# Gated delta rule beside two dense projections: the recurrence of eight heads as two staggered chains of four

## The chip, the cores and the metric

The kernel runs on one core of one Trainium2 chip. Its metric is the device time of one execution in microseconds, as the median of three runs. A core has TensorE (PE, with its weight loads shown apart as PEld), VectorE (DVE), ScalarE (ACT), GpSimd (POOL) and SyncE (SP, which here only issues DMAs). Each engine works through its own instructions in a fixed order.

## The reference, cut to what matters

One decoder layer: RMSNorm, one wide input projection, three mixers beside each other (gated DeltaNet, stick-breaking attention, memory attention), each projected to 1024 channels, gated and summed, then an output projection, residual and RMSNorm. The part in question is the recurrence of the DeltaNet mixer and what it feeds:

```
def step(s, xs):                      # 8 heads, dk = dv = 128
    q_n, w_n, u_n, k_n, a_n, last_n = xs
    v_new = u_n - einsum('bhcd,bhde->bhce', w_n, s)
    o = einsum('bhcd,bhde->bhce', q_n, s) + einsum('bhcs,bhse->bhce', a_n, v_new)
    s = s * exp(last_n) + einsum('bhcd,bhce->bhde', k_n, v_new)
    return s, o
...
o_dn = merge_heads(rmsnorm(o_dn, dn_norm_g)) * silu(dn_z)
merged = g_dn * (o_dn @ w_br_dn) + g_sb * (o_sb @ w_br_sb) + g_m * (o_m @ w_br_mem)
```

The state `s` of a head at chunk n needs chunk n-1 of the same head, and nothing of the other heads.

## The kernel before, in words

All data are 32 bit. The big projections are done as three products each of a high and a low part (`mm3`, and the three matmuls of `branch`), over tiles of 128 by 512. Up to about 1220 us of the execution the kernel does the input projection, the triangular solves, memory attention and stick-breaking attention. Then comes the stage in question. It has two things to do at once:

- **The dense branches** (`branch`, L1125 and on). For each of 8 blocks of 128 output channels and both halves of the 1024 tokens: first the memory branch (`y_ym`, contraction over 2 tiles), then the stick-breaking branch (`y_ysb`, over 8 tiles), at last the delta branch (`y_ydn`, over 8 tiles, one for each head of the recurrence). The sums gather in `mer`. Each result takes one of four PSUM banks of the tag `y` until DVE has multiplied it with its gate `gt` (L1143, or L1145 and L1146).
- **The recurrence** (`recurrence`), over 8 chunks n of 128 tokens and, within a chunk, two groups g of four heads. One chunk of one group is a chain: `kS` (L775, keys times state), `vb` (L777, DVE), `Tr` (L783, the solved triangle times `vb`), `vn` (L785, ACT), then `o` (L790 and L791, the output) and `dS` (L795, the change of state), `S` (L798, DVE), and a last part that norms `o` (ACT L808, POOL L809 to L811, DVE L812), transposes it (`oT`, L815), multiplies it with the gate `zt` (L816) and splits it into `odnh` and `odnl` (L143, L144), which `y_ydn` reads. `kS`, `Tr`, `o` and `dS` go to three PSUM banks of the tag `wk`. Each of their 128 by 128 matmuls is in plain 32 bit and shows as two matmuls in the trace.

What orders the two against each other: `recurrence` is a generator that yields between the parts of a chain, and `branch` calls `beside3` after every second contraction tile (40 calls in the memory and stick-breaking branches), which advances the generator to a share `RP` = 1.05 of its 65 steps, some 1.7 steps for each call. What is left after the last call is drained before the delta branch. The program so recorded is then ordered once more, when it is built, by a scheduler with its own timing model: each engine's instructions get a fixed order, and may stand elsewhere than in the program. Loads are issued by SP, in order too. A load into a buffer that is still read waits on SP for its release, and all later loads wait behind it.

The loads of a chunk (`loads`) are `kt`, `vb`, `tt` (three pieces), `kd`, `qd`, `at` and `zt`. `kd`, `qd` and `zt` have one buffer for both groups, `kt`, `vb` and `at` have two.

At the start of the stage the last tiles of stick-breaking attention (`av`, `aTp`, `aTl`) still run. The memory branch's input is `om` times `zm` (L1119, in `raw_m`), split into `oh_m` and `ol_m`, its weights are split into `w_wbm`, and the attention's outputs are loaded into `raw_sb` and split into `oh_sb` and `ol_sb`, through four `raw` buffers.

Of the kernel before, what the change touches and what calls it, by code (L numbers as in the profile page):

```python
# [11 lines left out]
F32 = mybir.dt.float32  # L12
F32R = mybir.dt.float32r
AF = mybir.ActivationFunctionType
ALU = mybir.AluOpType
# [4 lines left out]
P = 128  # L20
T = 1024
NT = 8
KC = 8
H = 8
# [13 lines left out]
def hybrid_block(ctx, tc, x, mem, norm_g, mem_norm_g, wq, wv0, wba, convw, a_log, dt_bias,  # L38
                 dn_g, wmk, wmv, wbd, wbs, wbm, wout, final_g, out):
    nc = tc.nc  # L40
    ve, sc, gp, pe, sy = nc.vector, nc.scalar, nc.gpsimd, nc.tensor, nc.sync
# [14 lines left out]
    cst = pool("cst", 1)  # L56
# [16 lines left out]
    def psum(tag, name):  # L73
        if tag == "X" and "X" not in banks["tags"]:
            tag = "z"
        if tag in MM:
            return mmp.tile([P, 512], F32, tag=tag, bufs=MM[tag], name=name)
        return banks["pool"].tile([P, 512], F32, tag=tag, bufs=banks["tags"][tag], name=name)
# [3 lines left out]

    ident = cst.tile([P, P], F32, name="ident")
    make_identity(nc, ident)
    tri = cst.tile([P, P], F32, name="tri")
    gp.memset(tri, 1.0)
    gp.affine_select(out=tri, in_=tri, compare_op=ALU.is_ge, fill=0.0, base=0,
                     pattern=[[1, P]], channel_multiplier=-1)
    ones = cst.tile([P, P], F32, name="ones")
    gp.memset(ones, 1.0)  # L90
    mhalf = cst.tile([P, 8], F32, name="mhalf")
    gp.memset(mhalf, -0.5)
    cw = cst.tile([P, 24, 4], F32, name="cw")
# [3 lines left out]
    def tab(n):  # L97
        if n not in tabs:
            tabs[n] = cst.tile([P, H, NT], F32, name="tab_" + n)
        return tabs[n]  # L100
# [163 lines left out]
    bat = cst.tile([P, NT, 16], F32, name="bat")  # L264
# [131 lines left out]
    v_st.close()  # L396


    beta, G, nG, eG, elast, dec = (tab(n) for n in ("beta", "G", "nG", "eG", "elast", "dec"))
    nr2, r1, r3, eq = tab("nr2"), tab("r1"), tab("r3"), tab("eq")  # L400
    SS = dict(c=None)

# [336 lines left out]
    def recurrence(ep, odn):  # L739
# [10 lines left out]
        def loads(n, g):  # L750
            kt = ld(kt_d, n, g, "kt") if n else None
            vb = ld(vb_d, n, g, "vb")
            tt, hs = tts[g], slice(g * 4, g * 4 + 4)
            for b in range(2):
                q = slice(b * 64, b * 64 + 64)
                sy.dma_start(out=tt[q, :, q], in_=td_d[b, hs, n].rearrange("h j i -> j h i"))
            sy.dma_start(out=tt[0:64, :, 64:P], in_=xx_d[n, :, hs, :])
            kd = ld(kd_d, n, g, "kd", 1) if n < NT - 1 else None
            qd = ld(qd_d, n, g, "qd", 1) if n else None
            at = ld(at_d, n, g, "at")  # L760
            zt = ep.tile([P, 4, P], F32, tag="zt", bufs=1, name=f"zt_{n}_{g}")
            sy.dma_start(out=zt, in_=zf_d[g * 4:g * 4 + 4, :, n * P:n * P + P].rearrange("h d t -> d h t"))
            return kt, vb, tt, kd, qd, at, zt

        ahead = loads(0, 0)
        yield
        for n in range(NT):
            for g in range(2):
                hs = range(4)
                kt, vb, tt, kd, qd, at, zt = ahead or loads(n, g)  # L770
                ahead = None
                if n:
                    o = psum("wk", f"kS_{n}_{g}")
                    for h in hs:
                        pe.matmul(o[:, h * P:h * P + P], kt[:, h, :], S[:, g * 4 + h, :], start=True, stop=True)  # L775
                    for h in hs:
                        ve.scalar_tensor_tensor(out=vb[:, h, :], in0=o[:, h * P:h * P + P],  # L777
                                                scalar=r3[:, g * 4 + h, n:n + 1], in1=vb[:, h, :],
                                                op0=ALU.mult, op1=ALU.add)
                    yield  # L780
                o = psum("wk", f"Tr_{n}_{g}")
                for h in hs:
                    pe.matmul(o[:, h * P:h * P + P], tt[:, h, :], vb[:, h, :], start=True, stop=True)  # L783
                vn = ep.tile([P, 4, P], F32, tag="vn", bufs=1, name=f"vn_{n}_{g}")
                sc.activation(vn, o.rearrange("p (h c) -> p h c", h=4), AF.Copy)  # L785
                yield
                oo = psum("wk", f"o_{n}_{g}")
                for h in hs:
                    if n:
                        pe.matmul(oo[:, h * P:h * P + P], qd[:, h, :], S[:, g * 4 + h, :], start=True, stop=False)  # L790
                    pe.matmul(oo[:, h * P:h * P + P], at[:, h, :], vn[:, h, :], start=(n == 0), stop=True)  # L791
                if n < NT - 1:
                    o = psum("wk", f"dS_{n}_{g}")
                    for h in hs:
                        pe.matmul(o[:, h * P:h * P + P], kd[:, h, :], vn[:, h, :], start=True, stop=True)  # L795
                    for h in hs:
                        if n:
                            ve.scalar_tensor_tensor(out=S[:, g * 4 + h, :], in0=S[:, g * 4 + h, :],  # L798
                                                    scalar=elast[:, g * 4 + h, n:n + 1],
                                                    in1=o[:, h * P:h * P + P], op0=ALU.mult, op1=ALU.add)  # L800
                        else:
                            ve.tensor_copy(S[:, g * 4 + h, :], o[:, h * P:h * P + P])
# [10 lines left out]
                o = psum("tr", f"oT_{n}_{g}")  # L813
# [2 lines left out]
                ve.tensor_tensor(out=zt, in0=o.rearrange("p (h c) -> p h c", h=4), in1=zt, op=ALU.mult)  # L816
                split([t[:, g * 4:g * 4 + 4, n * P:n * P + P] for t in odn], zt)
                yield

    SOLVE, MEM, COMB, RECUR = 1 + 1 + 62 + 8, 4 * 6, 16, 1 + 16 * 4  # L820

# [62 lines left out]

    b_st = sub()
    bp = pool("B", 1, stack=b_st, side="right")
    def hn(t):
        return t.rearrange("p h n -> p n h")

# [405 lines left out]
```

## Time and profile before

| | |
|---|---|
| median of 3 runs | 1628.51 us (1625.81 to 1630.97) |
| the profiled execution | 1621.97 us, its span from first to last instruction 1620.3 us |
| PE busy | 1549.0 us, 96% of the span |
| weight loads | 1299.1 us, 80% |
| DVE, ACT, POOL busy | 1180.3 us (73%), 819.6 us (51%), 312.5 us (19%) |
| granted TensorE clock, mean | 0.986 of full speed |
| moved by DMA | 223.32 MB, mean 138 GB/s |

PE is busy nearly throughout, so the few places in which it stands still are what can be taken away. A share of busy time over the whole span hides them; the rows below look at the stage from 1235 to 1442 us alone.

### The profile page before, as it was taken

Reading aid. Unit: us, or ns where it says so; the run is one execution under the profiler, and the core shown is the slowest. Engines: PE = TensorE matmul, PEld = TensorE weight load, DVE = VectorE, ACT = ScalarE, POOL = GpSimd, SP = SyncE. Lnnn points to the kernel's source line nnn. Section 1 sums busy time; section 2 is a strip of 40 time slices with the busy share of each in tenths; the row PEclk is TensorE's granted clock in tenths of the full one; section 3 lists DMA queues with packets and bytes.
Section 4 is the critical chain, followed back from the end, with each engine's and each line's share of the span. In section 5 each row is a group of like instructions: output and inputs, shape, how many; then the busy total and the mean of one; then the engine's idle time right before and its main releaser. Section 6 shows DMA issues by size and latency. Waiting matters only on the chain.

```text
span 1620.3 us, 23277 instructions
## 1 busy us (share of the span) xinstructions
PE 1549.0 (96%) x7979; PEld 1299.1 (80%) x7979; DVE 1180.3 (73%) x1903; ACT 819.6 (51%) x1909; POOL 312.5 (19%) x567
## 2 busy tenths in 40 slices
PE   6899999999999998998999999999998999979998
PEld 6888888887888776776788888888886888868786
DVE  8688989879999997553587778878867755544333
ACT  7578877765555435544455545545554322232121
POOL 4516445331113200000011111111110110110011
PEclk9999999999999998998999999999999999999999
DMA  8337556563333465233322322332138966644232
GB/s 290 97 106 222 160 154 195 164 201 100 109 104 118 143 195 168 83 111 86 119 78 92 103 79 90 107 105 79 66 124 255 304 195 181 206 126 133 82 104 78
DMA packets 152359, 223.32 MB, mean 138 GB/s; under 512 B 39984, under 2 KB 68144, under 8 KB 151984
## 3 DMA queue, kind: packets, MB, share of 16 engines
q1 hardware_dynamic: 107424, 159.94, 32.7%
q10 hardware_dynamic: 35712, 32.51, 6.1%
q0 software_dynamic: 9104, 29.37, 5.4%
q8 instruction: 63, 1.03, 0.3%
q14 instruction: 56, 0.46, 0.1%
HBM read 150.36 MB, written 71.40 MB: 137 GB/s over the span
## 4 chain that ended last, share of the span: by engine, by line
PE 83%; DVE 6%; DMA 5%; ACT 3%; issue 2%; SPq 0%; POOL 0%; ACTq 0%; DVEq 0%; POOLq 0%
PE mmY_g L160 3%; PE mmY_g L162 3%; PE mmY_g L161 3%; PE mmY_skq L160 2%; PE aTp L1033 2%; PE mmY_skq L161 2%; PE mmY_skq L162 2%; PE out L1203 2%; PE out L1201 2%; PE out L1202 2%; PE y_ydn L1135 2%; PE y_ydn L1136 2%; PE y_ydn L1137 2%; PE y_ysb L1136 2%; PE y_ysb L1135 2%
## 5 line engine op out<-in xcount | busy, mean ns | idle before, releaser
L1007 DVE TENSOR_TENSOR_SCAN pf<-pf 128x512 f32<-128x512 f32 (+4 forms) x96 | 97.1, 1012 | 15.7 <-POOL pf L1005 15.7
L143 ACT ACTIVATE aTh<-aTp 128x512 fp32r<-128x512 f32 (+2 forms) x96 | 44.6, 497 | 62.8 <-PE aTp L1033 59.5
L144 DVE TENSOR_TENSOR aTl<-aTp,aTh 128x512 fp32r<-128x512 f32 (+2 forms) x96 | 50.5, 546 | 25.7 <-ACT aTh L143 25.7
L992 POOL MEMSET pf<- 128x1 f32 x64 | 6.0, 98 | 327.0 <-PE aTp L1033 181.0
L1005 POOL TENSOR_SCALAR_AFFINE_SELECT pf<-pf 128x128 f32<-128x128 f32 x64 | 26.5, 415 | 204.7 <-ACT pf L1001 204.7
L1001 ACT ACTIVATE pf<-z 128x512 f32<-128x512 f32 (+4 forms) x96 | 47.1, 498 | 28.6 <-PE z L162 24.9
L1010 DVE TENSOR_TENSOR pf<-be,pf 128x512 f32<-128x512 f32 (+4 forms) x96 | 53.4, 557 | 3.7
L651 DVE TENSOR_TENSOR M<-M,tmp 128x62 f32<-128x62 f32 (+30 forms) x62 | 53.5, 863 | 0.3
L648 DVE TENSOR_TENSOR tmp<-M 128x62 f32<-128x62 f32 (+30 forms) x62 | 53.2, 858 | 0.2
L1201 PE MATMUL out<-oh_wo,mh 128*128 128x512 f32 x128 | 50.0, 391 | 1.5 <-ACT mh L143 1.5
L1135 PE MATMUL y_ydn<-odnh,w_ydn 128*128 128x512 f32 x128 | 49.5, 391 | 1.7 <-ACT odnh L143 1.7
L1049 PE MATMUL av<-aTl,vh 128*128 128x256 f32 (+1 forms) x160 | 47.0, 294 | 3.8 <-DVE aTl L144 3.7
L1135 PE MATMUL y_ysb<-oh_sb,w_ysb 128*128 128x512 f32 x128 | 50.6, 395 | 0.0
L1137 PE MATMUL y_ysb<-oh_sb,w_ysb 128*128 128x512 f32 x128 | 50.5, 395 | 0.0
L1136 PE MATMUL y_ysb<-ol_sb,w_ysb 128*128 128x512 f32 x128 | 50.3, 393 | 0.0
L1137 PE MATMUL y_ydn<-odnh,w_ydn 128*128 128x512 f32 x128 | 49.9, 390 | 0.0
L1136 PE MATMUL y_ydn<-odnl,w_ydn 128*128 128x512 f32 x128 | 49.8, 389 | 0.0
L1202 PE MATMUL out<-ol_wo,mh 128*128 128x512 f32 x128 | 49.8, 389 | 0.0
L1002 ACT ACTIVATE be<-z 128x512 f32<-128x512 f32 (+4 forms) x96 | 47.3, 503 | 4.2 <-DVE pf L1010 4.0
L1203 PE MATMUL out<-oh_wo,ml 128*128 128x512 f32 x128 | 49.3, 389 | 0.0
L1048 PE MATMUL av<-aTh,vh 128*128 128x256 f32 (+1 forms) x160 | 45.2, 283 | 1.4 <-ACT aTh L143 1.4
L1208 DVE TENSOR_TENSOR xo<-out,xo 128x512 f32<-128x512 f32 x16 | 11.0, 691 | 48.0 <-PE out L1203 48.0
(818 smaller groups left out, 5535.4 us busy)
## 6 DMA issues: line engine op xcount, KB each, us to landing
wb_g_b<-in_wq_dram SPq DMA_DIRECT2D x48, 256.0 KB, 2.8
wb_kq_b<-in_wq_dram SPq DMA_DIRECT2D x32, 256.0 KB, 3.0
wb_skq_b<-in_wq_dram SPq DMA_DIRECT2D x32, 256.0 KB, 2.7
g_d<-g ACTq DMA_DIRECT2D x32, 256.0 KB, 2.0
xt<-in_x_dram SPq DMA_DIRECT2D x8, 512.0 KB, 4.6
wb_sz_b<-in_wq_dram SPq DMA_DIRECT2D x16, 256.0 KB, 3.6
kt_d<-kq ACTq DMA_DIRECT2D x16, 256.0 KB, 3.4
gam<-gr_d SPq DMA_DIRECT2D x8, 512.0 KB, 4.4
```

What stands on the lines that cost most here:

```text
L160: pe.matmul(o, ah, bh, start=(first and i == 0), stop=False, **kw)
L161: pe.matmul(o, ah, bl, start=False, stop=False, **kw)
L162: pe.matmul(o, al, bh, start=False, stop=(i == n - 1), **kw)
L651: ve.tensor_tensor(out=d, in0=d, in1=t, op=ALU.add)
L1007: ve.tensor_tensor_scan(out=pv[:, ::-1], data0=pv[:, ::-1], data1=pv[:, ::-1], initial=pf[:, off + c1:off + c1 + 1], op0=ALU.mult, op1=ALU ...
L1010: ve.tensor_tensor(out=d, in0=be, in1=d, op=ALU.mult)
L1135: pe.matmul(oo[hf], wh, oh[:, s], start=(k == 0), stop=False)
L1136: pe.matmul(oo[hf], wh, ol[:, s], start=False, stop=False)
L1137: pe.matmul(oo[hf], wl, oh[:, s], start=False, stop=(k == n - 1))
L1201: pe.matmul(oo[hf], mh[:, k, :], wo[k][0][:, s], start=(k == 0), stop=False)
L1202: pe.matmul(oo[hf], mh[:, k, :], wo[k][1][:, s], start=False, stop=False)
L1203: pe.matmul(oo[hf], ml[:, k, :], wo[k][0][:, s], start=False, stop=(k == KC - 1))
```

## The change

Each group of four heads becomes a generator of its own, `chain(g)`, of four steps for each chunk: (0) loads, `kS`, `vb`; (1) `Tr`, `vn`; (2) `dS`, `o`, `S`; (3) norm, `oT`, gate, split. Chain 1 runs two steps behind chain 0, and the steps of the two alternate, so that between two steps of one chain there stands one of the other. Within step 2, `dS` now stands ahead of `o`. `zt` gets a second buffer. To make room for it, the constants `tri` and `ones` move into a pool that is closed early, and the tables `G` and `nG` move into the space of `bat`, which is not read any more by then.

```diff
-    beta, G, nG, eG, elast, dec = (tab(n) for n in ("beta", "G", "nG", "eG", "elast", "dec"))
+    beta, eG, elast, dec = (tab(n) for n in ("beta", "eG", "elast", "dec"))
+    G, nG = (bat.rearrange("p n c -> p (n c)")[:, j * 64:j * 64 + 64].rearrange("p (h n) -> p h n", h=H)
+             for j in range(2))
...
-            zt = ep.tile([P, 4, P], F32, tag="zt", bufs=1, name=f"zt_{n}_{g}")
+            zt = ep.tile([P, 4, P], F32, tag="zt", bufs=2, name=f"zt_{n}_{g}")
...
-        ahead = loads(0, 0)
-        yield
-        for n in range(NT):
-            for g in range(2):
-                hs = range(4)
+        def chain(g, ahead=None):
+            hs = range(4)
+            for n in range(NT):
                 kt, vb, tt, kd, qd, at, zt = ahead or loads(n, g)
...
-                    yield
+                yield
...
+                if n < NT - 1:
+                    o = psum("wk", f"dS_{n}_{g}")
+                    for h in hs:
+                        pe.matmul(o[:, h * P:h * P + P], kd[:, h, :], vn[:, h, :], start=True, stop=True)
                 oo = psum("wk", f"o_{n}_{g}")
...
                 if n < NT - 1:
-                    o = psum("wk", f"dS_{n}_{g}")
-                    for h in hs:
-                        pe.matmul(o[:, h * P:h * P + P], kd[:, h, :], vn[:, h, :], start=True, stop=True)
...
+        first_loads = loads(0, 0)
+        yield
+        two = chain(0, first_loads), chain(1)
+        for i in range(4 * NT + 2):
+            for g in (1, 0):
+                if 0 <= i - 2 * g < 4 * NT:
+                    next(two[g])
+                    yield
```

The scheduler's order of the two programs is the same up to the end of stick-breaking attention, but for the constants. In names such as `kS_6_1` the first number is the chunk, the second the group, and the last a running number.

PE, near the end of the recurrence, before (chunk 6, both groups):

```order
L795 MATMUL dS_6_0_13952<-vn_6_0_13941,kd_6_0_13887 128x128 x4
L775 MATMUL kS_6_1_14006<-S_12452,kt_6_1_13991 128x128 x4
L783 MATMUL Tr_6_1_14027<-vb_6_1_13993,tt1_12454 128x128 x4
L790 MATMUL o_6_1_14046<-S_12452,qd_6_1_14000 128x128
L815 MATMUL oT_6_0_13983<-ident_66,sq_6_0_13973 128x128 x4
L791 MATMUL o_6_1_14046<-vn_6_1_14032,at_6_1_14002 128x128
```

And after, at chunk 7:

```order
L770 MATMUL kS_7_0_14107<-S_12450,kt_7_0_14094 128x128 x4
L1149 MATMUL y_ysb_6_1_14063<-oh_sb_7_12952,w_ysb_6_1_14055 128x512
L1147 MATMUL y_ysb_7_0_14233<-oh_sb_0_12533,w_ysb_7_0_14221 128x512
L1148 MATMUL y_ysb_7_0_14233<-ol_sb_0_12534,w_ysb_7_0_14221 128x512
L1149 MATMUL y_ysb_7_0_14233<-oh_sb_0_12533,w_ysb_7_0_14221 128x512
L1147 MATMUL y_ysb_7_1_14234<-oh_sb_0_12533,w_ysb_7_0_14221 128x512
```

Before, from `Tr_6_0` to the end of the recurrence no dense matmul stood between its parts: `Tr` came right behind the `kS` that it needs. After, 21 dense matmuls stand between `kS_7_0` and `Tr_7_0` (the last blocks of the stick-breaking branch), 12 between the first and second product of `o_7_0`, and 24 between `Tr_7_1` and `o_7_1`.

DVE, at the end of stick-breaking attention, before:

```order
L1010 TENSOR_TENSOR pf_7_0_12414<-be_7_0_0_12420,pf_7_0_12414 128x128
L1119 TENSOR_TENSOR raw_m_1_1_12493<-raw_m_1_1_12493,raw_zm_1_1_12495 128x512
L144 TENSOR_TENSOR aTl_7_1_12430<-aTp_7_1_0_12431,aTh_7_1_12429 128x2x128
L144 TENSOR_TENSOR aTl_7_1_12430<-aTp_7_0_0_12500,aTh_7_1_12429 128x128
L144 TENSOR_TENSOR ol_m_1_12485<-raw_m_1_1_12493,oh_m_1_12484 128x512
L144 TENSOR_TENSOR w_wbm0_0_12527<-raw_wbm0_0_12525,w_wbm0_0_12527 128x512
```

And after:

```order
L138 TENSOR_TENSOR aTl_7_1_12428<-aTp_7_1_0_12429,aTh_7_1_12427 128x2x128
L138 TENSOR_TENSOR aTl_7_1_12428<-aTp_7_0_0_12498,aTh_7_1_12427 128x128
L1131 TENSOR_TENSOR raw_m_1_1_12491<-raw_m_1_1_12491,raw_zm_1_1_12493 128x512
L138 TENSOR_TENSOR ol_m_1_12483<-raw_m_1_1_12491,oh_m_1_12482 128x512
L138 TENSOR_TENSOR w_wbm0_0_12525<-raw_wbm0_0_12523,w_wbm0_0_12525 128x512
```

The product for the memory branch's last input piece (`raw_m_1_1`) moved behind the two `aTl`, which come from PE.

ACT, in the first blocks of the memory branch, before:

```order
L143 ACTIVATE oh_sb_3_12696<-raw_sb_3_1_12702 128x512
L785 ACTIVATE vn_0_0_12568<-Tr_0_0_12563 128x512
L143 ACTIVATE w_wbm4_0_12746<-raw_wbm4_0_12744 128x512
L143 ACTIVATE w_wbm4_1_12751<-raw_wbm4_1_12749 128x512
L143 ACTIVATE oh_sb_4_12754<-raw_sb_4_0_12756 128x512
```

And after:

```order
L137 ACTIVATE oh_sb_3_12662<-raw_sb_3_1_12668 128x512
L137 ACTIVATE w_wbm4_0_12712<-raw_wbm4_0_12710 128x512
L137 ACTIVATE w_wbm4_1_12717<-raw_wbm4_1_12715 128x512
L137 ACTIVATE oh_sb_4_12720<-raw_sb_4_0_12722 128x512
L780 ACTIVATE vn_0_0_12596<-Tr_0_0_12591 128x512
```

`vn_0_0` moved behind three splits of freshly loaded data, and on PE the step that it feeds (`dS_0_0`, `o_0_0`, `Tr_0_1`) moved from behind the memory branch's block 2 to just ahead of the last matmul of block 3. On SP the loads of chunk 1 (`vb_1_0`, `tt0`) and `kd_0_1` moved behind the last `raw_wbm` and further `raw_sb`, and `zt_0_1` moved to an early place, ahead of the memory branch's `raw_zm_1_1`.

## Rows read from the trace of the kernel before

**Rows 1.** The windows view of the stage, one line for each stretch: its length, then busy time and instructions of PE, weight loads, DVE, ACT and POOL, the granted TensorE clock, the DMA engines' mean share, GB/s.

```profile
1235.00:1263.00 28.00, 24.15 (x134) 19.86 (x133) 18.88 (x33) 12.54 (x34) 2.93 (x6) 1.00 0.92 273
1263.00:1402.00 139.00, 138.96 (x819) 122.24 (x818) 78.54 (x171) 36.59 (x117) 14.12 (x27) 1.00 0.70 218
...
1412.00:1420.00 8.00, 4.90 (x42) 4.47 (x40) 4.47 (x9) 3.29 (x12) 0.23 (x1) 1.00 0.62 194
1420.00:1425.00 5.00, 4.24 (x22) 4.24 (x23) 2.77 (x8) 1.16 (x2) 1.23 (x2) 0.66 0.77 228
1425.00:1442.00 17.00, 11.38 (x91) 10.47 (x90) 7.84 (x19) 5.72 (x29) 3.95 (x9) 1.00 0.49 134
1442.00:1520.00 78.00, 78.00 (x348) 64.54 (x347) 33.97 (x52) 15.38 (x24) 0.85 (x1) 1.00 0.35 108
```

**Rows 2.** The timeline of PE from 1411 us to 1442 us: start, duration, line, out<-in, and in brackets the idle time before it with what ended it.

```profile
1411.57 1.05 PE L783 MATMUL Tr<-vb,tt 128*128 128x128 f32 x8
1412.46 0.39 PE L790 MATMUL o<-S,qd 128*128 128x128 f32 x2
...
1414.56 0.49 PE L791 MATMUL o<-vn,at 128*128 128x128 f32 x2 [1.27 <-ACT vn L785]
...
1417.11 1.06 PE L775 MATMUL kS<-S,kt 128*128 128x128 f32 x8
1420.76 1.64 PE L783 MATMUL Tr<-vb,tt 128*128 128x128 f32 x8 [2.59 <-DVE vb L777]
...
1428.22 1.26 PE L783 MATMUL Tr<-vb,tt 128*128 128x128 f32 x8 [0.58 <-DVE vb L777]
1431.01 0.49 PE L790 MATMUL o<-S,qd 128*128 128x128 f32 x2 [1.53 <-DMA qd<-qd_d]
...
1437.05 0.49 PE L790 MATMUL o<-S,qd 128*128 128x128 f32 x2 [1.76 <-DMA qd<-qd_d]
...
1441.29 0.74 PE L1135 MATMUL y_ydn<-odnh,w_ydn 128*128 128x512 f32 x2 [1.75 <-ACT odnh L143]
```

**Rows 3.** The timeline of PE at the start of the stage.

```profile
1235.29 0.44 PE L1135 MATMUL y_ym<-oh_m,w_wbm 128*128 128x512 f32 x1
...
1244.09 0.47 PE L1135 MATMUL y_ym<-oh_m,w_wbm 128*128 128x512 f32 x1 [1.82 <-DVE mer L1143]
...
1246.90 1.05 PE L791 MATMUL o<-vn,at 128*128 128x128 f32 x8
1247.79 1.06 PE L795 MATMUL dS<-vn,kd 128*128 128x128 f32 x8
1248.68 1.06 PE L783 MATMUL Tr<-vb,tt 128*128 128x128 f32 x8
1249.49 0.48 PE L1135 MATMUL y_ym<-oh_m,w_wbm 128*128 128x512 f32 x1
...
1255.57 0.50 PE L1135 MATMUL y_ym<-oh_m,w_wbm 128*128 128x512 f32 x1 [1.71 <-DVE mer L1143]
```

**Rows 4.** The timeline of DVE there.

```profile
1231.86 0.68 DVE L1119 TENSOR_TENSOR raw_m<-raw_m,raw_zm 128x512 f32<-128x512 f32 x1
1233.98 0.62 DVE L144 TENSOR_TENSOR aTl<-aTp,aTh 128x256 fp32r<-128x256 f32 x2 [1.45 <-ACT aTh L143]
...
1247.64 0.69 DVE L144 TENSOR_TENSOR w_wbm<-raw_wbm,w_wbm 128x512 fp32r<-128x512 f32 x1 [1.30 <-ACT w_wbm L143]
1248.26 1.28 DVE L1143 TENSOR_TENSOR mer<-y_ym,gt_ym 128x512 f32<-128x512 f32 x2
...
1256.96 0.69 DVE L812 TENSOR_TENSOR sq<-o,so 128x512 f32<-128x512 f32 x1 [0.66 <-POOL so L811]
```

**Rows 5.** The timeline of ACT there.

```profile
1234.00 0.63 ACT L143 ACTIVATE oh_m<-raw_m 128x512 fp32r<-128x512 f32 x1
1234.52 1.15 ACT L143 ACTIVATE w_wbm<-raw_wbm 128x512 fp32r<-128x512 f32 x2
...
1245.51 0.58 ACT L785 ACTIVATE vn<-Tr 128x512 f32<-128x512 f32 x1
1246.98 0.63 ACT L143 ACTIVATE w_wbm<-raw_wbm 128x512 fp32r<-128x512 f32 x1 [0.89 <-DMA raw_wbm<-in_wbm_dram]
1251.08 0.63 ACT L143 ACTIVATE w_wbm<-raw_wbm 128x512 fp32r<-128x512 f32 x1 [3.47 <-DMA raw_wbm<-in_wbm_dram]
1252.11 0.63 ACT L143 ACTIVATE oh_sb<-raw_sb 128x512 fp32r<-128x512 f32 x1 [0.40 <-DMA raw_sb<-osb_d]
...
1254.09 0.26 ACT L808 ACTIVATE sq<-o 128x128 f32<-128x128 f32 x1
```

**Rows 6.** The tile view of `qd` over the whole span, its last line: from the issue of a load to its landing.

```profile
DMA to landing us min/median/max: 2.7/3.8/5.5
```

**Rows 7.** The waits of SP's own queue from 1200 us to 1460 us: who waited for whom, in total, times, longest.

```profile
SPq L747 <- PE o L791: 16.4, 9, 3.4
SPq L762 <- DVE odnl L144: 13.6, 7, 6.7
SPq L1092 <- DVE w_ysb L144: 11.4, 9, 2.8
```

**Rows 8.** The timeline of POOL where the constants now go.

```profile
80.85 1.88 POOL L899 TENSOR_TENSOR ea<-ea,al 128x8 f32<-128x8 f32 x1 [4.42 <-DMA al<-in_a_log_dram]
...
100.58 0.76 POOL L931 TENSOR_SCALAR tab_nG<-tab_G 128x64 f32<-128x64 f32 x1 [0.58 <-DVE tab_G L930]
```

More of the change, by code (lines that the diff above doesn't have):

```diff
@@ L84, in hybrid_block @@
     make_identity(nc, ident)
[L85 to L90, printed above, removed]
     mhalf = cst.tile([P, 8], F32, name="mhalf")
@@ L886, in hybrid_block @@
     bp = pool("B", 1, stack=b_st, side="right")
+    tri = bp.tile([P, P], F32, name="tri")
+    gp.memset(tri, 1.0)
+    gp.affine_select(out=tri, in_=tri, compare_op=ALU.is_ge, fill=0.0, base=0,
+                     pattern=[[1, P]], channel_multiplier=-1)
+    ones = bp.tile([P, P], F32, name="ones")
+    gp.memset(ones, 1.0)
     def hn(t):
```

## The prediction

> **What bounds the kernel now.** I read the windows of the stage first, then PE's timeline, then the engines that PE waits for. From 1263 to 1402 us PE is busy for 138.96 of 139 us, and again for all of 1442 to 1520 us, at full clock [rows 1]. There the recurrence's steps are already hidden among dense matmuls, and only fewer matmuls would help; the change has the same number. So its worth lies where PE stands still. That is in two places. From 1412 to 1442 us PE is idle for 3.10 + 0.76 + 5.62 = 9.48 us (8.00 less 4.90, 5.00 less 4.24, 17.00 less 11.38), and the granted clock is 0.66 from 1420 to 1425 us [rows 1]. In PE's timeline these are six waits, 1.27, 2.59, 0.58, 1.53, 1.76 and 1.75 us, which sum to the same 9.48 [rows 2]. The reader is to see what each waits for: the next part of a chain whose last part has only just run (`vn`, `vb`, then `odnh`), or a `qd` that could not be loaded before its buffer was free. It is the latency of a chain with nothing left to do beside it. The second place is the start, from 1235 to 1263 us: 28.00 less 24.15 is 3.85 us idle, most of it two waits of 1.82 and 1.71 us for a PSUM bank that DVE has not yet emptied [rows 3]. The DMA engines are 0.92 busy there [rows 1], and ACT waits for what they bring [rows 5].
>
> **The tail: what the change removes.** In the new order dense matmuls stand between the parts of the last chunks. One costs 78.00 / 348 = 0.224 us [rows 1], and a step of eight small ones 0.89 us (1246.90 to 1247.79 to 1248.68) [rows 3].
> - `kS_7_0` to `Tr_7_0`: 21 dense, 4.7 us. Before, `Tr` waited 2.59 and 0.58 us behind `kS` [rows 2], so the need is at most 0.89 less than 1420.76 - 1417.11, or 2.8 us. Covered.
> - `Tr_7_0` to the first product that needs `vn`: 12 dense, 2.7 us, and `kS_7_1` and a transpose besides. Before: from 1412.46, where `Tr` was through, to 1414.56 with 1.27 us of waiting [rows 2]. Covered.
> - `qd_7_1`, whose buffer is free when `o_7_0` ends: `Tr_7_1` and 24 dense, 0.89 + 5.4 = 6.3 us, against 2.7 to 5.5 us from issue to landing, median 3.8 [rows 6]. Covered, unless SP issues it late.
> - The end: from `o_7_1` to `oT_7_1` 37 dense (8.3 us), against 3.6 us from the first square on ACT (1254.09) to the end of the normed product on DVE (1256.96 + 0.69) [rows 4, 5]; then 23 dense (5.2 us) before the first `y_ydn` that reads heads 4 to 7.
>
> So all six waits go: 9.48 us. What also goes is the slow clock. At 0.66 over 5 us, PE ran 3.4 us at 1.2 GHz in place of 2.4 [rows 1], which doubles what it did then: 1.7 us. Together 11.2 us. What is late next there is DVE's and ACT's own work for the delta branch, which the trace of before doesn't show in this place; between nothing and a return of the last two waits (about 3 us) I take 0.5, since the stretch to 1402 us, built in the same manner, shows 0.04 us of idleness in 139 [rows 1].
>
> **The start: what the change adds.** DVE now does `raw_m` times `raw_zm` behind the two `aTl`. Before, it ran at 1231.86, in a hole; `aTl` ends at 1234.60 [rows 4]. The product then ends at 1235.3, and `oh_m`, which ACT began at 1234.00, begins 1.3 us later, and with it `w_wbm` and the first dense matmul (1235.29) [rows 3, 5]. The `raw_sb` loads, which wait for the same buffers, shift with it. Price: **1.3 us**.
>
> Next, `o_0_0`, `dS_0_0` and `Tr_0_1` stood between blocks 2 and 3 of the memory branch and kept PE busy from 1246.90 to 1249.49 [rows 3]. They now stand behind block 3, whose bank DVE empties only after `w_wbm` (1247.64), in the first of two products from 1248.26, so at about 1248.9 [rows 4]. PE gets there 2.6 us sooner and stands from 1246.90 to 1248.9: **2.0 us**, all shifted by the same 1.3.
>
> On ACT `vn_0_0` moves from 1245.51 behind two `w_wbm` and an `oh_sb` that wait for data until 1252.11 [rows 5]. `dS_0_0` is reached at 1248.9 + 11 x 0.224 = 1251.4 (both shifted), against `vn` at some 1253.3; but the loads that it waits behind also come ahead of four recurrence loads now, and with DMA 0.92 busy that is worth about as much. I take nothing, and up to 1.5 us as the bad end. The wait of 1.71 us at 1255.57 goes; two of about 1 us, an estimate from the 1.82 and 1.71, I expect in its place, where block 5 waits for a bank behind `ol_sb`, and `oT_0_0` behind a weight split: **0.3 us**. Sum of the start 3.6 us; 0 if the earlier loads make up for all, 6.5 with `vn` late (1.5) and one more fall of the clock as in the tail (1.7).
>
> The clock bears on this. After 1.27 and 2.59 us of waiting within nine, it was 0.66; after single waits of 1.82 and 1.71 us, eleven apart, it stayed at 1.00 [rows 1 to 3]. The start now has more of them close together. The Trainium skill, page TensorE: Matmul & The Clock Gate, section What's actually happening, says that the slow clock is the default and that activity releases it; by that rule closer waits would cost the start 1.7 us more, and by the rows nothing is certain.
>
> **The rest.** `tri` and `ones` are now made just ahead of `ea`, where POOL has 4.42 us idle up to 80.85, long before `G`, which comes of them, is read at 100.58 [rows 8]: nothing. `G` and `nG` in `bat` change names alone. The second `zt` frees SP from its wait for `odnl` (13.6 us in 7) [rows 7], which held later loads back; PE waited for none of that before 1402 us, so it is worth nothing by itself. Of the steps between 1263 and 1402 us none loses its cover: 15 to 24 dense matmuls, 3.4 us or more, stand between any two parts of one chain.
>
> **Sum.** -11.2 + 0.5 + 3.6 = -7.1 us. On the profiled execution, 1621.97 us, that is 1614.9. That execution lies below all three timed runs, so against the median the same difference gives 1628.51 - 7.1 = **1621.4 us**.
>
> **The rivals.** *The start eats it.* With the start at its bad end and 1 to 1.5 us of late work in the tail, the gain is 11.2 - 6.5 - 1.5 = 3.2 us: 1625.3. For it: the DMA engines are nearly full there, and ACT and DVE wait in order behind loads [rows 1, 5]. Against it: loads that PE needs first now come first.
>
> *The waits only change places.* The chains would be as bare as before, only later, beside the delta branch, whose second half needs the last chunk: about 1628. Against it stands the new order, with 21, 12 and 24 dense matmuls in between.
>
> *Slower, by `kd` and `qd`.* They still have one buffer, and within a chunk group 1 now has less time to load: from `o_n_0` to `o_n_1` only 0.89 + 23 x 0.224 + 0.89 = 6.9 us, where a turn took half a chunk. A landing of 5.5 us [rows 6] and two issues leave about 0.6 us. SP was held by `w_ysb` for up to 2.8 us [rows 7]; in front of `qd` that would cost PE 2.2 us in each of seven chunks, 15 us, and so 1621.4 + 15 = 1636. It decides from (7.1 + 4.9) / 7 = 1.7 us for each chunk. Against it: the median landing, 3.8 us, leaves 2.3.
>
> **How the numbers follow.** 0.3% is 4.9 us, about what a measurement of this kernel can tell from no change; it puts the bounds at 1623.6 and 1633.4. Forecast 0.62, the start eats it 0.27, the waits change places 0.05, slower 0.06. So faster 0.62, same 0.32, slower 0.06. The low end has both costs at nothing, 1617.3, less half the spread of the three runs (2.6): 1614.7. The high end has the start at 6.5 and 3 us back in the tail, 1626.8, and the same 2.6: 1629.4, which takes in the first two rivals.
>
> **What would show it.** Right: no waits for `vb`, `vn` or `qd` in the last 40 us before the delta branch, clock 1.00 there, the first dense matmul of the memory branch about 1.3 us later against the end of attention, a wait of about 2 us ahead of its block 3, and no idleness in between. Wrong: waits of PE for `kd` or `qd` in each chunk; a clock under 1.00 at the start; or waits for `odnh` or `w_ydn` beside the delta branch.

## The result, and the profile after

The changed kernel takes 1618.91 us (median of 6 runs, 1615.0 to 1622.85) against 1628.64 us before (6 runs, 1625.81 to 1630.97): a ratio of 0.9941, 95% interval 0.9921 to 0.9961, or 9.7 us less (6.4 to 12.9). That is faster by over 0.3%. A second series, run with the experiments below, gave medians of 1616.93 against 1625.09 us, 8.2 us less, and a ratio of 0.9941 again. (The ratios here are worked out over all executions of a series and are not the quotients of the medians, which would be 0.9950 in this series.)

The two profiled executions differ by only 0.5 us (1621.49 and 1621.97). In that of the changed kernel the last transposition of stick-breaking attention began at 1240.04 us, in that of before at 1232.88. These 7.16 us were lost ahead of that attention, whose first transposition began at 820.26 us against 813.14, where the engines' orders are alike: the mean clock was 0.92 against 0.94 from 600 to 813 us. In the other kernels below that first transposition began anywhere from 813.8 to 821.5 us, so scatter is enough to explain it, without any price of the moved constants. So I compare what the change touches by itself: **the stage** from that transposition to the first matmul of the output projection, with the same 1530 matmuls in both. The windows view of the kernel before, over its stage (columns as in [rows 1]):

```profile
1232.88:1524.73 291.85, 276.91 (x1530) 238.42 (x1530) 156.21 (x311) 80.30 (x232) 24.76 (x48) 0.99 0.61 186
```

And of the changed kernel, piece by piece and, in the last line, over its stage:

```profile
1240.04:1243.59 3.55, 2.68 (x10) 1.89 (x10) 1.76 (x4) 1.75 (x5) 0.00 (x0) 0.50 0.47 152
1243.59:1273.40 29.81, 24.99 (x119) 19.74 (x120) 19.55 (x34) 12.45 (x27) 1.46 (x3) 0.94 0.89 272
1273.40:1299.00 25.60, 24.57 (x147) 21.25 (x146) 16.95 (x37) 7.75 (x26) 2.94 (x6) 1.00 0.99 299
1299.00:1402.00 103.00, 103.00 (x658) 92.69 (x657) 59.84 (x135) 28.09 (x102) 13.12 (x27) 1.00 0.70 211
1402.00:1442.00 40.00, 40.00 (x244) 35.54 (x243) 23.25 (x48) 13.73 (x48) 5.83 (x12) 1.00 0.55 171
1442.00:1524.18 82.18, 81.14 (x360) 66.88 (x358) 36.91 (x57) 16.96 (x26) 0.00 (x0) 1.00 0.34 109
1240.04:1524.18 284.14, 276.38 (x1530) 237.97 (x1530) 158.24 (x312) 80.73 (x232) 23.35 (x48) 0.99 0.62 190
```

The stage fell from 291.85 to 284.14 us, by 7.71 (of the kernel before there is one profile only). PE's idle time in it (length less PE busy) fell from 14.94 to 7.76 us, by 7.18; the remaining 0.53 us are matmuls that ran faster or slower with the clock. Where 9.48 us of idleness and a clock of 0.66 stood before [rows 1], PE is now busy for 40.00 of 40 us at full clock. What idleness is left lies ahead of 1299 us, but for 1.04 us at the very end, which was there before too. The waits of PE over the stage, by what ended them (total, times, longest):

```profile
PE y_ym L1147 <- DVE mer L1155: 3.0, 4, 1.1
PE dS L785 <- DMA kd<-kd_d: 2.3, 2, 1.3
PE oT L811 <- DVE sq L808: 0.6, 1, 0.6
PE y_ym L1147 <- ACT w_wbm L137: 0.4, 1, 0.4
PE av L1060 <- ACT aTh L137: 0.4, 1, 0.4
```

No wait for `vb`, `vn`, `qd` or `odnh` is left; two waits for `kd` are new. PE's timeline where the six waits of [rows 2] stood:

```profile
1416.18 1.06 PE L770 MATMUL kS<-S,kt 128*128 128x128 f32 x8
...
1421.86 1.05 PE L778 MATMUL Tr<-vb,tt 128*128 128x128 f32 x8
...
1424.08 0.39 PE L789 MATMUL o<-S,qd 128*128 128x128 f32 x2
...
1427.06 0.38 PE L790 MATMUL o<-vn,at 128*128 128x128 f32 x2
...
1434.98 0.38 PE L789 MATMUL o<-S,qd 128*128 128x128 f32 x2
```

`Tr` now stands 5.68 us behind the `kS` that it needs, the product with `vn` 5.2 us behind `Tr`, and not one of these lines has a bracket: the data were there. And PE's timeline at the start, for [rows 3]:

```profile
1240.04 0.86 PE L1045 MATMUL aTp<-ident,pf 128*128 128x128 f32 x3
...
1243.59 0.80 PE L1147 MATMUL y_ym<-oh_m,w_wbm 128*128 128x512 f32 x1 [0.45 <-ACT w_wbm L137]
1244.18 0.63 PE L1148 MATMUL y_ym<-ol_m,w_wbm 128*128 128x512 f32 x1
1244.61 0.63 PE L1149 MATMUL y_ym<-oh_m,w_wbm 128*128 128x512 f32 x1
...
1252.45 0.47 PE L1147 MATMUL y_ym<-oh_m,w_wbm 128*128 128x512 f32 x1 [0.46 <-DVE mer L1155]
...
1257.12 0.50 PE L1147 MATMUL y_ym<-oh_m,w_wbm 128*128 128x512 f32 x1 [1.08 <-DVE mer L1155]
...
1272.18 1.13 PE L785 MATMUL dS<-vn,kd 128*128 128x128 f32 x8 [1.28 <-DMA kd<-kd_d]
...
1297.82 1.13 PE L785 MATMUL dS<-vn,kd 128*128 128x128 f32 x8 [1.03 <-DMA kd<-kd_d]
```

The first dense matmul comes 3.55 us behind the last transposition, against 2.41 before (1235.29 [rows 3] less 1232.88). And it runs at half speed: the next ones start 0.43 us apart (1244.18 to 1244.61), where before they were 0.23 us apart from the fourth on. PE stood idle for only 0.45 us ahead of it.

### The profile page after: what moved, and what is told of

The parts are those of the page before. It is cut to its first block, busy times and chain, and to the rows that moved or that the text cites. A ratio compares the mean times of both kernels' runs of the same rounds, so it can differ in the third digit from the quotient of the medians.

```text
span 1619.7 us, 23278 instructions
## 1 busy us (share of the span) xinstructions
PE 1553.3 (96%) x7979; PEld 1302.4 (80%) x7979; DVE 1182.5 (73%) x1903; ACT 820.4 (51%) x1909; POOL 315.5 (19%) x567
## 3 DMA queue, kind: packets, MB, share of 16 engines
q8 instruction: 63, 1.03, 0.3%
## 4 chain that ended last, share of the span: by engine, by line
PE 66%; issue 4%; DMA 3%; DVE 3%; ACT 1%; POOL 1%; SPq 0%; POOLq 0%; DVEq 0%; ACTq 0%
PE mmY_g L154 3%; PE mmY_g L156 3%; PE mmY_g L155 3%; PE mmY_skq L154 2%; PE mmY_skq L155 2%; PE mmY_skq L156 2%; PE y_ydn L1149 2%; PE y_ydn L1148 2%; PE out L1215 2%; PE y_ydn L1147 2%; PE out L1213 2%; PE out L1214 2%; PE aTp L1045 2%; PE y_ysb L1147 2%; PE y_ysb L1148 2%
## 5 line engine op out<-in xcount | busy, mean ns | idle before, releaser
L1062 PE MATMUL av<-aTh,vl 128*128 128x256 f32 (+1 forms) x160 | 46.2, 289 | 0.0
```

## The experiments

Twelve runs follow, of ten further kernels and of two kernels a second time. My theory was that of the prediction: the two chains put dense matmuls between the parts of the last chunks, and that is the whole gain; the second `zt` buffer is worth nothing. Besides the ratio to the kernel before (measured beside it in the same series), the table has from each profile: how long behind the last transposition the first dense matmul begins, the mean clock over the first 45 us, the stage, and PE's idle time in it.

| kernel | first dense | clock, 45 us | stage | idle | ratio (95% interval) |
|---|---|---|---|---|---|
| before | 2.41 | 0.99 | 291.85 | 14.94 | 1 |
| changed | 3.55 | 0.92 | 284.14 | 7.76 | 0.9941 (0.9921, 0.9961) |
| after_again (the same) | 3.56 | 0.92 | 283.25 | 6.91 | 0.9941 (0.9921, 0.9961) |
| zt2_only | 3.56 | 0.92 | 298.94 | 14.98 | 1.0035 (1.0023, 1.0047) |
| chains_zt1 | 2.41 | 0.99 | 279.72 | 6.40 | 0.9926 (0.9913, 0.9939) |
| zt1_again (the same) | 2.91 | 0.88 | 281.72 | 4.83 | 0.9916 (0.9888, 0.9944) |
| zt2_held | 2.24 | 0.96 | 279.40 | 5.09 | 0.9918 (0.9889, 0.9948) |
| chains_ds_last | 3.56 | 0.92 | 284.89 | 7.42 | 0.9960 (0.9948, 0.9972) |
| chains_kd2 | 3.56 | 0.95 | 283.51 | 7.59 | 0.9961 (0.9950, 0.9972) |
| zt1_pace08 | 2.91 | 0.93 | 291.09 | 12.20 | 1.0018 (1.0003, 1.0033) |
| zt1_apart8 | 3.62 | 0.95 | 282.39 | 6.60 | 0.9924 (0.9898, 0.9950) |
| zt_later | 2.02 | 0.92 | 285.94 | 11.00 | 0.9941 (0.9920, 0.9961) |
| raw5 | 2.97 | 0.94 | 287.29 | 10.00 | 0.9964 (0.9949, 0.9980) |
| zt1_sblate | 2.16 | 0.96 | 280.39 | 6.50 | 0.9928 (0.9902, 0.9954) |

The attention ahead of the stage (from its first to its last transposition 418.6 to 420.1 us) and what follows the stage (95.5 to 95.6 us to the last instruction) are alike in all of them.

### Which part of the change it is

**zt2_only**: the kernel before, with the second `zt` buffer and the space made for it.

```diff
-            zt = ep.tile([P, 4, P], F32, tag="zt", bufs=1, name=f"zt_{n}_{g}")
+            zt = ep.tile([P, 4, P], F32, tag="zt", bufs=2, name=f"zt_{n}_{g}")
```

> The kernel before with two buffers for zt and the space for them, and nothing else. I compare the stage from the last transposition of stick-breaking attention to the first matmul of the output projection: 291.85 us in the kernel before, 284.14 in the changed one. Theory (the gain comes from the two chains alone): the six waits of the tail stay, 9 to 10 us of idleness, stage 291 to 292.5 us, ratio 0.999 to 1.001. Rival (the second buffer frees SP, so that qd comes earlier): the two waits for qd, 3.3 us, and the slow clock behind them, 1.7 us, go: stage about 287 us, ratio about 0.997.

Neither came: it is slower, by 0.35%, and its stage is 7.1 us longer. The waits of the tail are all there (`qd` 3.4 us, `vb` 3.3, `odnh` 1.8), so the rival falls. The windows view of its tail and of its stage:

```profile
1417.00:1452.00 35.00, 25.84 (x168) 23.60 (x167) 15.87 (x36) 10.19 (x42) 6.27 (x12) 0.85 0.49 148
...
1236.41:1535.35 298.94, 283.96 (x1530) 242.86 (x1530) 156.78 (x312) 80.89 (x232) 23.87 (x48) 0.97 0.58 180
```

Idle time is as before (14.98 against 14.94 us); the whole loss is PE busy time, 283.96 against 276.91, with a clock of 0.92 over the first 45 us and 0.85 in the tail (in the kernel before 0.99, and 0.95 from 1413.5 to 1448.5 us). Why the clock lay lower in the tail too, among waits of the same length, no run shows. The first dense matmul came at 3.56 us, as in the changed kernel. So this delay came with the buffer, without the chains.

**chains_zt1**: the other half, the two chains with one buffer.

```diff
-            zt = ep.tile([P, 4, P], F32, tag="zt", bufs=2, name=f"zt_{n}_{g}")
+            zt = ep.tile([P, 4, P], F32, tag="zt", bufs=1, name=f"zt_{n}_{g}")
```

> The changed kernel with one buffer for zt again: the two chains without the buffer. Theory: stage 283.5 to 285 us as with the buffer (284.14), ratio 0.993 to 0.995, since PE never waits for anything that SP issues behind zt. Rival (the chains need the buffer): SP, held by zt until the split into odnl, issues kd and qd late, PE waits 1 to 2 us in four or more chunks: stage 288 us or more, ratio 0.997 or more.

The rival is out, and the theory was too modest: the stage is 4.4 us shorter than with the buffer, the ratio 0.9926. The tail has no waits, and the first dense matmul is back at 2.41 us. The chains alone make the gain; by these two profiles the buffer takes part of it back (the intervals of the ratios overlap; more on it below).

**chains_ds_last**: `dS` behind `o` again.

```diff
-                if n < NT - 1:
-                    o = psum("wk", f"dS_{n}_{g}")
-                    for h in hs:
-                        pe.matmul(o[:, h * P:h * P + P], kd[:, h, :], vn[:, h, :], start=True, stop=True)
                 oo = psum("wk", f"o_{n}_{g}")
...
                 if n < NT - 1:
+                    o = psum("wk", f"dS_{n}_{g}")
+                    for h in hs:
+                        pe.matmul(o[:, h * P:h * P + P], kd[:, h, :], vn[:, h, :], start=True, stop=True)
```

> The changed kernel with dS behind o again, as before. Theory: the 0.9 us by which S comes later in each chunk lies beside 12 or more dense matmuls (2.7 us): stage 283.5 to 285.5 us, ratio 0.993 to 0.996. Rival (the order within the step carries the gain, because S ends the chain that sets the pace): seven chunks by 0.9 us, stage about 290 us, ratio about 0.998.

As the theory said: 284.89 us, idle 7.42, no wait in the tail. Its one large wait is `dS` for `kd`, 3.2 us, at the start.

### The single buffers of kd and qd

**chains_kd2**: the second buffer goes to `kd`, and `zt` has one.

```diff
-            kd = ld(kd_d, n, g, "kd", 1) if n < NT - 1 else None
+            kd = ld(kd_d, n, g, "kd", 2) if n < NT - 1 else None
...
-            zt = ep.tile([P, 4, P], F32, tag="zt", bufs=2, name=f"zt_{n}_{g}")
+            zt = ep.tile([P, 4, P], F32, tag="zt", bufs=1, name=f"zt_{n}_{g}")
```

> The changed kernel with the second buffer given to kd in place of zt. Theory: the two waits of dS for kd (1.28 and 1.03 us), which are the whole price of the single buffers, go, and nothing comes in their place: stage 281.5 to 283 us, ratio about 0.992. Rival (kd was late because the DMA queues are full at the start, not for want of a buffer): dS or the dense branch waits as long for something else, stage 284 us, ratio 0.994.

The rival came. From the waits of PE over its stage:

```profile
PE oT L811 <- DVE sq L808: 1.9, 3, 0.8
PE y_ym L1147 <- DVE mer L1155: 1.3, 1, 1.3
...
PE o L789 <- DMA qd<-qd_d: 0.8, 1, 0.8
PE dS L785 <- ACT vn L780: 0.7, 1, 0.7
```

`kd` is gone from the list, and waits of 1.9, 0.8 and 0.7 us stand there instead, all in the first 60 us of the stage. It also begins its dense work at 3.56 us: here a load of `kd` is issued ahead of the last `raw_zm`, and the extra buffer of `kd` delays the start as much as one of `zt`.

### Is it the dense matmuls in between?

**zt1_pace08**: the chains with one buffer, spread thinner over the dense branches, so that little is left between their last parts.

```diff
-RP = 1.05
+RP = 0.8
```

> The two chains with one zt buffer (stage 279.72 us), with the pace RP at 0.8 in place of 1.05: the recurrence is spread thinner, so that the last chunk's parts have no dense matmul between them again, as in the kernel before, while the chains, their buffers and their matmuls are the same. Theory (the change gains by the dense matmuls that stand between the parts of the last chunks): six or so waits for vb, vn, qd and odnh return in the last 40 us ahead of the delta branch, 6 to 10 us in sum, with a clock below 1.00, stage 287 to 292 us, ratio about 0.998. Rival (the chains gain because two of them hide each other's latency, whatever lies between): waits of 2 us at most, stage 281 to 283 us, ratio about 0.994.

The theory's numbers: stage 291.09 us, 11.4 more than with RP at 1.05. From PE's timeline, all waits in the last 45 us ahead of the delta branch:

```profile
1426.00 0.63 PE L811 MATMUL oT<-ident,sq 128*128 128x128 f32 x4 [2.26 <-DVE sq L808]
1429.04 2.08 PE L785 MATMUL dS<-vn,kd 128*128 128x128 f32 x8 [2.42 <-ACT vn L780]
1434.71 1.26 PE L778 MATMUL Tr<-vb,tt 128*128 128x128 f32 x8 [0.45 <-DVE vb L772]
1441.23 0.49 PE L789 MATMUL o<-S,qd 128*128 128x128 f32 x2 [1.12 <-DMA qd<-qd_d]
1445.86 0.74 PE L1147 MATMUL y_ydn<-odnh,w_ydn 128*128 128x512 f32 x2 [1.84 <-ACT odnh L137]
```

Five waits, 8.1 us in sum: four for `vn`, `vb`, `qd` and `odnh`, as in [rows 2], and one for `sq`, a late part of a chain too. The same chains without dense matmuls between their parts lose all that they had gained. The other half of this test was not run: whether the kernel before, with its one sequence and a higher `RP`, would have covered its tail as well. So it is shown that the dense matmuls in between make the gain, and not that it takes two chains to get them there.

**zt1_apart8**: the second chain eight steps behind, in place of two.

```diff
-        for i in range(4 * NT + 2):
+        for i in range(4 * NT + 8):
             for g in (1, 0):
-                if 0 <= i - 2 * g < 4 * NT:
+                if 0 <= i - 8 * g < 4 * NT:
```

> The two chains with one zt buffer (stage 279.72 us), the second chain eight steps (two chunks) behind the first in place of two. Theory (how far apart they run does not matter, so long as the steps of both alternate and dense matmuls lie between): no waits of more than 1 us in the last 40 us ahead of the delta branch, stage 279 to 282 us, ratio 0.992 to 0.994. Rival (two steps are the distance that the buffers want: each buffer is then free half a chunk before its next use): waits for kd or qd in most chunks, 1 to 2 us each, stage 286 us or more.

The theory, with 0.4 us over its range: PE is busy for all of the last 130 us ahead of the output projection but its last 1.04, with no wait for `kd` or `qd`; the stage of 282.39 us has its 2 to 3 us more at the start (first dense at 3.62 us, one wait of 2.2 us for `vn`). The distance of two steps is not what counts. In this kernel too DVE does the last product of `raw_m` behind both `aTl`, at 1240.15 us, 1.70 us behind the last transposition, though `zt` has one buffer and no load of `zt` or `kd` goes ahead of the last `raw_zm`.

### What the start costs, and why

The new order of SP shows where the buffer acts. SP's timeline of the changed kernel:

```profile
1230.07 0.38 SPq L759 DMA_DIRECT2D zt<-zf_d  x1
1230.51 0.49 SPq L744 DMA_DIRECT2D kt<-kt_d  x1
1231.05 0.42 SPq L744 DMA_DIRECT2D qd<-qd_d  x1
1231.52 0.43 SPq L744 DMA_DIRECT2D kt<-kt_d  x1
1232.56 0.32 SPq L1104 DMA_DIRECT2D raw_zm<-zm_d  x1
```

With a free second buffer the load of `zt_0_1` (256 KB) is issued ahead of the last `raw_zm`. The build then also placed the DVE product that needs `raw_zm` later. DVE's timeline of the changed kernel, and then of chains_zt1:

```profile
1241.14 0.62 DVE L138 TENSOR_TENSOR aTl<-aTp,aTh 128x256 fp32r<-128x256 f32 x2 [2.05 <-ACT aTh L137]
1241.68 0.68 DVE L1131 TENSOR_TENSOR raw_m<-raw_m,raw_zm 128x512 f32<-128x512 f32 x1
```

```profile
1235.12 0.68 DVE L1131 TENSOR_TENSOR raw_m<-raw_m,raw_zm 128x512 f32<-128x512 f32 x1
1237.24 0.62 DVE L138 TENSOR_TENSOR aTl<-aTp,aTh 128x256 fp32r<-128x256 f32 x2 [1.45 <-ACT aTh L137]
```

Against the last transposition (1240.04 and 1236.14 us) the product starts 1.64 us behind it in the one and 1.02 us ahead of it in the other. In the changed kernel DVE stood idle for 2.05 us just before, and the data were there: this `raw_zm` landed 5.1 us from its issue (the tile view of that load), at 1237.7 us, 3.4 us ahead of the end of that idleness. In chains_zt1 it was issued at the same place, 7.47 us ahead of the last transposition against 7.48, and landed in 3.5 us. So the early `zt` may have delayed it by 1.6 us, but even then it was there 2.4 us ahead of the last transposition, early enough for the place that chains_zt1 gives the product. The load did not hold up the product; the fixed order did, which the build made, presumably reckoning with a later landing. zt1_apart8 shows that an early load is not the only thing that makes the build choose this order.

**zt_later**: both buffers, but `zt` is loaded in the last step of a chain, not with the rest.

```diff
-            sy.dma_start(out=zt, in_=zf_d[g * 4:g * 4 + 4, :, n * P:n * P + P].rearrange("h d t -> d h t"))
...
+                sy.dma_start(out=zt, in_=zf_d[g * 4:g * 4 + 4, :, n * P:n * P + P].rearrange("h d t -> d h t"))
                 ov = oo.rearrange("p (h c) -> p h c", h=4)
```

> The changed kernel, both buffers for zt kept, but a chunk's zt is loaded only in the last step of its chain, where it is read, and no longer with the other loads. So far every kernel with one more 2 KB buffer for the recurrence (zt or kd) began its first dense matmul 3.56 us behind the last transposition of attention, and those without it 2.40; the former also showed a granted clock of 0.92 to 0.95 over the first 45 us, against 0.99. Theory (the buffer costs because zt_0_1 is then loaded ahead of the last raw_zm, which lands some 2 us later, so that DVE's product comes behind the attention's two aTl): first dense matmul at 2.4 us or less, clock 0.98 or more there, stage 279 to 281 us, ratio about 0.993. Rival (the larger buffer itself, by where things then lie, or chance in the clock): first dense matmul at 3.56 us again, stage 283 to 285 us, ratio about 0.996.

Half right. The first dense matmul came at 2.02 us, but the stage took 285.94, since PE then met this, and later waited 4.0 us for `kd` as well:

```profile
1247.14 0.77 PE L1147 MATMUL y_ym<-oh_m,w_wbm 128*128 128x512 f32 x1 [4.51 <-DVE mer L1155]
```

In this kernel's order DVE has seven splits of attention outputs (`ol_sb`) ahead of the first product into `mer`, which empties the first PSUM bank, where the other kernels have five; each waits for a load. PE had filled its four banks and stood.

**raw5**: one buffer for `zt`, and a fifth for `raw`.

```diff
-        t = fp.tile([P, 512], F32, tag="raw", bufs=4, name="raw_" + nm)
+        t = fp.tile([P, 512], F32, tag="raw", bufs=5, name="raw_" + nm)
```

> The two chains with one zt buffer (stage 279.72 us), and the space given to a fifth buffer for raw, through which the memory branch's inputs, the attention outputs and the weights come. Theory (the waits of the first 45 us, 3.0 us for PSUM banks that DVE has not emptied, come of loads that arrive late): DVE and ACT get their data earlier, half of these waits goes, stage 277 to 279.5 us, ratio 0.991 to 0.993. Rival (the DMA engines are 0.92 busy there, so an earlier load only delays another, or DVE's own work is the bound): stage 279.5 to 281 us.

Worse than either said: 287.29 us. Earlier loads this time brought eight splits ahead of the first bank: PE waited 4.6 us for banks, 2.5 for `kd` and 1.3 for `vb`. My idea that earlier data help at the start fell with these two.

**zt1_sblate**: the attention's outputs one block later.

```diff
-        if i < 6:
-            osb += load_o(osb_d, [i], "sb")
+        if 0 < i < 7:
+            osb += load_o(osb_d, [i - 1], "sb")
```

> The two chains with one zt buffer, and the attention's outputs loaded and split one block of the memory branch later from block 1 on. Where loads came earlier than in this kernel (zt only in the last step, or a fifth raw buffer), DVE had 7 splits of attention outputs ahead of the first emptied bank in place of 5, each waiting for its load, and PE waited 4.5 us for that bank. Theory (these splits ahead of the products into mer are what makes PE wait for banks at the start, 3.0 us in the kernel with one zt buffer): with fewer of them ahead of the third and later products the waits for banks fall to 1 to 2 us, stage 278 to 279.5 us. Rival (the DMA engines, 0.92 busy there, are the bound): the waits move on to the weights or to kd, stage 279.5 to 281.5 us.

By the stage the rival, 280.39 us. The list of waits has none for a bank, and two of 2.5 and 1.3 us that are put down to ACT's split of the attention outputs (`oh_sb`). That is misleading, since neither matmul reads `oh_sb`. The lines of DVE and PE at the first:

```profile
1243.10 1.28 DVE L1155 TENSOR_TENSOR mer<-y_ym,gt_ym 128x512 f32<-128x512 f32 x2
1243.94 0.77 PE L1147 MATMUL y_ym<-oh_m,w_wbm 128*128 128x512 f32 x1 [2.49 <-ACT oh_sb L137]
```

The first of the two products into `mer` ends at about 1243.78, 0.16 us ahead of the matmul, much as in chains_zt1, where the same wait is put down to `mer` (1246.72 and 1246.86). And the `kd` of the second wait was issued at 1253.79 and landed 5.3 us later, at 1259.1; the matmul began at 1259.27. So the waits for a bank and for `kd` are still there, 2.5 and 1.3 us against 3.0 and 1.2 in chains_zt1: loading later neither removed them nor moved them.

**zt2_held**: both buffers, but the second is first written from the first chunk's `vn`, which keeps the early load out.

```diff
                 sc.activation(vn, o.rearrange("p (h c) -> p h c", h=4), AF.Copy)
+                if n == g == 0:
+                    hold = ep.tile([P, 4, P], F32, tag="zt", bufs=2, name="hold")
+                    gp.tensor_scalar(out=hold[:, 0, 0:4], in0=vn[:, 0, 0:4], scalar1=1.0, scalar2=None, op0=ALU.mult)
```

> The changed kernel with both zt buffers, but the second one is first written (four columns, by POOL) from the first chunk's vn, so that no zt can be loaded into it before the memory branch has begun. Every engine's order at the start is then that of the two chains with one buffer. Theory (the second buffer costs because zt_0_1 is loaded ahead of the last raw_zm of the memory branch): first dense matmul 2.4 us behind the last transposition, clock 0.98 or more over the first 45 us, stage 279 to 281 us, ratio about 0.993. Rival (the buffer itself costs, or SP's freedom later on): stage 283 to 286 us, ratio about 0.996.

The theory's numbers but for the clock (0.96, by one fall some 11 us into the stage): first dense at 2.24 us, stage 279.40 us, ratio 0.9918. The buffer itself costs nothing that shows here and gives nothing; the cost comes with its early load.

### The same kernels again

**after_again** and **zt1_again** have no edit against the changed kernel and chains_zt1.

> The changed kernel once more, for a second profile of its start. Theory (the low clock at the start follows from the late first dense matmul, 3.56 us behind the last transposition): it starts at 3.56 us again, and the clock over the first 45 us is 0.92 to 0.95 again, stage 283 to 285.5 us. Rival (the 10 us at half clock were an accident of the one profile): clock 0.98 or more, stage 279.5 to 281.5 us.

> The two chains with one zt buffer once more, beside the changed kernel on the same chip, as the version that may beat both. Theory: first dense matmul at 2.4 us, clock 0.98 or more over the first 45 us, stage 279 to 281 us, 3 to 5 us shorter than that of the changed kernel, ratio about 0.993. Rival (its short start was an accident): clock 0.92 to 0.95, stage 283 us or more.

The changed kernel did as the theory said (3.56 us, 0.92, 283.25 us). The other did not: it began without a wait, its stage was 281.72 us, and its clock lay low nearly as long as that of the changed kernel. The windows view of the first stretch, of chains_zt1 and then of zt1_again, two executions of one program:

```profile
1236.14:1247.00 10.86, 8.87 (x43) 6.79 (x44) 7.46 (x13) 6.25 (x12) 0.00 (x0) 0.95 0.80 257
```

```profile
1234.35:1245.00 10.65, 10.22 (x37) 8.14 (x38) 6.72 (x12) 5.87 (x11) 0.00 (x0) 0.67 0.77 248
```

So the low clock can last as long without the late product. Nor is the whole delay of the first dense matmul the product's: zt1_again, slow but without a wait, has 2.91 us, and the product makes it 3.55 to 3.62 whether the clock is low or not. In medians of one series the changed kernel took 1616.93 us, zt1_again 1612.95 and zt2_held 1613.59: without the early load 3.3 to 4.0 us less. The intervals of their ratios overlap, but set directly against each other the eleven executions of the changed kernel and the twelve of these two differ by 4.5 us in the mean, by their scatter 2.4 to 6.5. What of the early load costs this stays open: the delay of 1.14 us, the clock or the traffic. zt1_apart8 speaks against the late product as the whole reason, since it has the product late, no early load, and a ratio of 0.9924 (four executions, so the interval is wide). The five fastest here, 0.9916 to 0.9928 of the kernel before, all have the chains and no early load; zt_later and raw5, which lack it too, lose to the waits told above.

## Why the prediction was right, step by step

The forecast was 1621.4 us, from -7.1 us against the kernel before; 1618.91 and -9.7 us were measured, within the range and on the side that had 0.62. The stage's own difference, -7.7 us, is nearer to the sum; what the other 2 us are no profile shows, and they lie within the interval (6.4 to 12.9).

- **The tail, -9.48 us of waits and -1.7 us of slow clock: right.** No wait and a clock of 1.00 from 1402 to 1442 us. zt1_pace08 shows the reason to be the one given: take the dense matmuls away, and 8.1 us of such waits return.
- **Late work in the tail, 0.5 us: none came.**
- **The first dense matmul 1.3 us later: 1.14 us.** The size and the late product were right; what moved the product was not named.
- **"The second `zt` ... is worth nothing by itself": this step failed.** Held back, it is indeed worth nothing (279.40 us against 279.72 and 281.72). As the change has it, its load goes ahead of the last `raw_zm`, and with that the build moves the product behind the two `aTl`. I priced this move as the chains' doing; zt2_only has it without any chains. By the medians of one series the early load costs 3 to 4 us of a gain that could have been about 12.
- **2.0 us ahead of block 3 and 0.3 us of exchanged waits: mis-sized.** The waits for banks are 2.97 us in sum against 3.53 before [rows 3], 0.6 less in place of 2.3 more; the one ahead of block 3 is 1.08 us. PE reached these blocks later than I had reckoned, since its first nine dense matmuls took 0.43 us each in place of 0.27; that this is the reason is argued, not shown.
- **`kd`: priced at nothing in the forecast, it cost 2.3 us**, two waits (one, of 1.3 us, in after_again). The rival "slower by `kd` and `qd`" foresaw them in each of seven chunks, for want of a buffer. They come only while the DMA engines are full (0.89 and 0.99 busy from 1243.59 to 1299 us), and the buffer was not what they waited for: the `dS` before had ended by 1260.8 and 1288.2 us, SP issued the loads only at 1267.20 and 1291.61, behind others, and they landed in 4.8 and 6.1 us. chains_kd2 shows that a second buffer does not buy them off.
- **The clock at the start** was in the range's bad end and not in the sum. Idle time up to 1402 us rose from 4.42 to 6.72 us, by 2.3; of the change in busy time, -0.53, the tail should give -1.7, which leaves some +1.2 for the start's clock. Together 3.5 us, beside the 3.6 forecast: the sum of the start held by luck, with terms that did not hold. A clock under 1.00 at the start was one of the prediction's own signs of being wrong, and "no idleness in between" failed too: waits of 1.10, 0.58, 1.28 and 1.03 us stand between 1266 and 1299 us.
- **A slip in the sum:** the bad end of the start, 3.6 with 1.5 and 1.7, makes 6.8 us and not 6.5. The high end of the range and the first rival's time would be 0.3 us higher, which changes nothing here.

The rival "the start eats it" (0.27) was right that the start costs, and wrong in size (3.5 us, not 6.5); the waits did not change places into the delta branch.

## What to carry to other kernels

A chain of dependent steps beside dense work needs its last parts covered too: run independent chains beside each other so that all are done before the dense work is, and check it at the last chunk, not in the middle. A buffer more is not free even when it costs no time to fill: it lets its load go ahead of others and can move work on engines that never touch it, so look at what stands first in the queues of the nearest critical stretch. Where a profile's total hides such parts, compare one stretch between two fixed instructions.

## What was not expected of the hardware

Two executions of one program, with the same order and no wait of PE between the last attention matmuls and the dense ones, differed in how long TensorE stayed at 1.2 GHz after the waits of 1.76 and 0.43 us ahead: to about 1 us behind the last transposition in chains_zt1, to about 7 us in zt1_again, although PE was busy for 10.22 of the first 10.65 us there. Over the stage the same matmuls were busy for 276.89 us against 273.32, 3.6 us more. In zt2_only the same idle time as in the kernel before came with 7 us more of busy time, at a mean clock of 0.97 in place of 0.99. The Trainium skill, page TensorE: Matmul & The Clock Gate, section What's actually happening, says of a kernel's start that the number of slow matmuls varies between runs of the same kernel; these traces agree, with 1 and 7 us, and show it in the middle of a kernel. A single profile does not show what a wait costs in clock.
